# A down projection in seven products: sums left in their PSUM banks, and five steps of operands ready

## The chip, the core and the metric

The kernel runs on one core of a Trainium2 chip. TensorE multiplies matrices into PSUM, VectorE, ScalarE and POOL (GpSimd) do the rest, and SyncE's queue issues nearly all transfers. The metric is the time of one execution on the device, in microseconds (us).

## The reference

One layer of a bidirectional encoder over 1024 tokens of width 1024, in float32: a mixer, then a gated feed-forward block, then a last norm. The change touches only the end, the product of the gated activations with w_down, the addition to h and the last norm:

```
up = h @ w_up                                  # (1024, 5632)
conv = conv_b + sum_k conv_w[k] * padded[:, k:k + L]
gate, val = split(conv, 2)                     # each (1024, 2816)
y = h + (gelu(gate) * val) @ w_down            # w_down: (2816, 1024)
return rmsnorm(y, g_final)
```

## The kernel before

Each float32 operand is split into a high and a low part, by a ScalarE copy (L151) and a VectorE subtraction (L152), and each product of two operands is three matmuls: high by high, high by low, low by high.

The up projection runs over 22 blocks of 128 columns (`up_pair`); the gated block j is stored to DRAM as `adr[j]`. The down projection takes these blocks back as its stationary operand. It is a Strassen-Winograd scheme: both matrices are cut in two in each direction, and the four quarters of the result come out of seven products in place of eight. Rows 0 to 3 of the result (s = 0..3, 128 tokens each) and rows 4 to 7 are the two halves of the tokens, n = 0 and 1 the two halves of the columns.

Each product (`down(p, acc, ...)`) has KH = 11 steps m. A step loads one block of activations and one of weights (`d_<m>a`, `d_<m>b`, 256 KB each), splits both (`ringed`, a ring of 12 operands, so six steps ahead at most) and issues 12 matmuls: three for each of four banks. Products use the four banks `qa` or the four banks `qb`. `fresh` says whether the first matmul overwrites the bank; without it the product adds to what is there. Each product's operands are sums or differences of quarters. chain_a and chain_b hold them from one product to the next: begin_b and begin_a load two blocks for each step and subtract or add (L1223, L1219), and later products go on from there (L1228 in place, L1213 into the loaded tile).

Products one, two, five, six, seven, four and three run in this order. After product one, take_1 copies the banks to `u2` (ScalarE). Product two adds to the same banks; take_2 adds them to hb, the rows of h with the result (VectorE). Product five goes to qb; take_5 adds it. Product six overwrites qa; take_6 adds the banks to u2 (VectorE), and POOL adds u2 to three quarters of hb (L1329 to L1331). Product seven overwrites qa; take_7 adds it to hb. Product four adds to seven's banks, and its rows 4 to 7 are finished by out_rows; product three adds to five's banks, its last four steps are done bank by bank (tail 4), and rows 0 to 3 are finished by out_rows: addition, squares, rstd_of, POOL's product with g_final (L1291), scaling, store.

The operands of the first three steps of product one are loaded by load_first while the last up block is computed, in buffers of their own (`first`). Steps three and on take theirs from the pool that follows, whose memory comes free only with the up projection's. All loads of weights and blocks keep the order of the program on SyncE's queue (`st_load`). The order of instructions on each engine is fixed when the program is built, by a planner with its own simulated times; an engine runs its list in order.

Of the kernel before, what the change touches and what calls it, by code (L numbers as in the profile page):

```python
# [11 lines left out]
F32 = mybir.dt.float32  # L12
F32R = mybir.dt.float32r
I32 = mybir.dt.int32
BF16 = mybir.dt.bfloat16
AF = mybir.ActivationFunctionType
# [4 lines left out]
P = 128  # L21
L = 1024
D = 1024
NS = 8
# [9 lines left out]
NWP = 5  # L34
# [47 lines left out]
def bc(ap, axis, n):  # L82
    ap = ap.unsqueeze(axis)
    shape = list(ap.shape)
    shape[axis] = n
    return ap.broadcast_to(shape)
# [3 lines left out]
def encoder_block(  # L90
# [8 lines left out]
    V, A, PE, GP = nc.vector, nc.scalar, nc.tensor, nc.gpsimd  # L99
# [5 lines left out]
    outer = ctx.enter_context(tc.tile_pool(name="outer", bufs=1))  # L105
# [10 lines left out]
    def bank(name):  # L116
        return ps.tile([P, 512], F32, name=name, tag="bank_a")

    def bank2(name):
        return ps.tile([P, 512], F32, name=name, tag="bank_b")  # L120
# [8 lines left out]
    def mm(o, lhsT, rhs, start, stop, key=None, skip=False):  # L129
        i = PE.matmul(o, lhsT, rhs, start=start, stop=stop, skip_group_check=skip)  # L130
        last_mm[0] = i
        if key is not None:
            if key in chain:
                after(i, chain[key])
            chain[key] = i
        return i
# [13 lines left out]
    def split(dst_hi, dst_lo, src, eng=V):  # L150
        A.activation(dst_hi, src, AF.Copy)  # L151
        return eng.tensor_sub(dst_lo, src, dst_hi.bitcast(F32))  # L152
# [3 lines left out]
    def st_load(i):  # L156
        if st_chain:
            after(i, st_chain[-1])
        st_chain.append(i)

    def load_split(src, a, name, w=None, eng=V, g=None, geng=None):

        st = outer.tile([P, 512], F32, name=name + "_st", tag="st", bufs=5)
        sv = st.rearrange("p (a b) -> p a b", a=a) if a > 1 else st
        st_load(nc.sync.dma_start(sv, src))
        if g is not None:
            if geng == "A":
                for k in range(a):
                    A.activation(sv[:, k], sv[:, k], AF.Copy, scale=g[:, k:k + 1])
            else:  # L170
                geng.tensor_mul(sv, sv, bc(g, 2, P))
        if w is None:
            w = outer.tile([P, 2, 512], F32R, name=name, tag="wp", bufs=NWP)
        split(w[:, 0], w[:, 1], st, eng)
        return w.rearrange("p t (a b) -> p t a b", a=a) if a > 1 else w
# [7 lines left out]
    def rstd_of(ss, name, parts=0):  # L183

        v = const.tile([P, 1], F32, name=name + "_v", tag="rs_v", bufs=4)
        V.tensor_scalar(v, ss[:, 0:1], -0.5 / D, -0.5 * EPS, ALU.mult, ALU.add)
        for i in range(1, parts):
            V.tensor_scalar(v, ss[:, i:i + 1], -0.5 / D, v, ALU.mult, ALU.add)  # L188
        y = const.tile([P, 1], F32, name=name + "_y", tag="rs_y", bufs=4)
        t = const.tile([P, 1], F32, name=name + "_t", tag="rs_t", bufs=4)  # L190
        V.tensor_scalar(y.bitcast(I32), v.bitcast(I32), -0.5, float(0x5F3759DF - 0x40400000), ALU.mult, ALU.add)  # L191
        for _ in range(3):
            V.tensor_scalar(t, y, y, v, ALU.mult, ALU.mult)  # L193
            V.tensor_scalar(y, t, 1.5, y, ALU.add, ALU.mult)  # L194
        return y
# [770 lines left out]
    def cv_tile(name):  # L966
        return fp.tile([P, L], F32, name=name, tag="cv", bufs=2)
# [7 lines left out]
    for n in range(2):  # L975
        ns_ = slice(n * 512, (n + 1) * 512)
        for m in range(4):
            pg = bank(f"pg{m}_{n}")
            first = True
            for k in range(4):  # L980
                for wi, zi in ((0, 0), (0, 1), (1, 0)):
                    mm(pg, wg[k][:, wi, m * P:(m + 1) * P], zf[:, k, zi, ns_],
                       start=first, stop=(k == 3 and wi == 1))
                    first = False
# [78 lines left out]
    def halves(name):  # L1063
        t = cv_tile(name)
        return t[:, 0:512], t[:, 512:1024]
# [93 lines left out]
    first = []  # L1159
# [33 lines left out]
    def ringed(t, name):  # L1193
        w = pb.tile([P, 2, 512], F32R, name=name, tag="wr", bufs=12)
        split(w[:, 0], w[:, 1], t)
        return w
# [51 lines left out]
    hbs = {}  # L1248
    ss3 = {}
# [4 lines left out]
        ss3[s] = pb.tile([P, 4], F32, name=f"n3_{s}_s2")  # L1254

    def step(p, m):
        if p == 1 and m < 3:
            return first[2 * m], first[2 * m + 1]
        return tuple(ringed(f(m, f"d{p}_{m}{'ab'[i]}"), f"d{p}_{m}{'ab'[i]}o") for i, f in enumerate(forms[p]))

    def down(p, acc, fresh, more, extra=None, tail=1, done=None):

        groups = [(m,) for m in range(KH - tail)] + [tuple(range(KH - tail, KH))]
        for ms in groups:
            ops = []
            for m in ms:
                ops.append((m, *step(p, m)))
                if extra is not None:
                    extra(m)
            for si in range(4):  # L1270
                for m, a, w in ops:
                    for ai, wi in ((0, 0), (0, 1), (1, 0)):
                        mm(acc[si], a[:, ai, si * P:(si + 1) * P], w[:, wi], start=(fresh and m == 0 and ai == 0 and wi == 0),
                           stop=(m == KH - 1 and ai == 1), skip=more)
                if done is not None and ms[-1] == KH - 1:
                    done(si)

    def hv(s, n):
        return hbs[s][:, n * 512:(n + 1) * 512]

    def squares(s, n):
        sq = pb.tile([P, 512], F32, name=f"n3_{s}_sq{n}", tag="sq", bufs=2)
        A.activation(sq, hv(s, n), AF.Square, accum_out=ss3[s][:, n:n + 1])

    def out_rows(s, late, acc):

        end = s == 3
        o = pb.tile([P, L], F32, name=f"o{s}", tag="o", bufs=3)
        early = 1 - late
        el, ll = (slice(512 * n, 512 * n + 512) for n in (early, late))  # L1290
        GP.tensor_mul(o[:, el], hv(s, early), gl[:, el])  # L1291
        if end:
            for i, (c0, c1) in enumerate(((512, 768), (768, 1024))):
                V.tensor_add(hbs[s][:, c0:c1], hbs[s][:, c0:c1], acc[:, c0 - 512:c1 - 512])
                sq = pb.tile([P, 512], F32, name=f"n3_{s}_sq{2 + i}", tag="sq", bufs=2)
                A.activation(sq[:, 0:256], hbs[s][:, c0:c1], AF.Square, accum_out=ss3[s][:, 1 + i:2 + i])  # L1296
            r = rstd_of(ss3[s], f"n3_{s}", 3)
            A.activation(o[:, el], o[:, el], AF.Copy, scale=r)  # L1298
            nc.scalar.dma_start(ov[s][:, el], o[:, el])
            V.scalar_tensor_tensor(o[:, ll], hv(s, late), r, gl[:, ll], ALU.mult, ALU.mult)  # L1300
            nc.sync.dma_start(ov[s][:, ll], o[:, ll])
            return
        V.tensor_add(hv(s, late), hv(s, late), acc)
        squares(s, late)
        r = rstd_of(ss3[s], f"n3_{s}", 2)
        A.activation(o[:, el], o[:, el], AF.Copy, scale=r)
        V.scalar_tensor_tensor(o[:, ll], hv(s, late), r, gl[:, ll], ALU.mult, ALU.mult)  # L1307
        nc.sync.dma_start(ov[s], o)

    u2 = [h for i in range(2) for h in halves(f"du{i}")]  # L1310
    qa = [bank(f"dqa{si}") for si in range(4)]
    qb = [bank2(f"dqb{si}") for si in range(4)]

    def add_to(s, n, t):
        V.tensor_add(hv(s, n), hv(s, n), t)

    def take_1(si):
        A.activation(u2[si], qa[si], AF.Copy)

    def take_2(si):  # L1320
        add_to(si, 0, qa[si])
        squares(si, 0)

    def take_5(si):
        add_to(4 + si, 1, qb[si])

    def take_6(si):
        V.tensor_add(u2[si], u2[si], qa[si])
        GP.tensor_add(hv(4 + si, 0), hv(4 + si, 0), u2[si])  # L1329
        GP.tensor_add(hv(4 + si, 1), hv(4 + si, 1), u2[si])  # L1330
        GP.tensor_add(hv(si, 1), hv(si, 1), u2[si])  # L1331

    def take_7(si):
        add_to(4 + si, 1, qa[si])
        squares(4 + si, 1)

    def with_1(m):
        if m < 6:
            begin_b(m)
# [14 lines left out]
        if m % 2 and m < 8:  # L1354
            load_row(4 + m // 2)

    def after_6(si):
        take_5(si)
        take_6(si)

    down(1, qa, True, True, with_1, 1, take_1)
    down(2, qa, False, True, with_2)
    down(5, qb, True, True, with_5, 1, take_2)
    down(6, qa, True, False, with_6, 1, after_6)
    down(7, qa, True, True, None, 1, take_7)
    down(4, qa, False, True, None, 1, lambda si: out_rows(4 + si, 0, qa[si]))
    down(3, qb, False, True, None, 4, lambda si: out_rows(si, 1, qb[si]))


_INS = ['x', 'g_mix', 'w_in', 'ssm_lam_re', 'ssm_lam_im', 'ssm_log_dt', 'ssm_b_re', 'ssm_b_im', 'ssm_c_re',  # L1370
# [58 lines left out]
```

## Time and profile before

| | |
|---|---|
| median of 3 runs | 1081.42 us (1079.25 to 1083.48) |
| profiled execution | 1079.52 us, span 1077.7 us |
| TensorE (PE) | busy 975.3 us, 90% |
| VectorE (DVE) | busy 945.1 us, 88% |
| ScalarE (ACT) | busy 464.6 us, 43% |
| POOL | busy 252.2 us, 23% |

The span runs from the first to the last instruction in the trace. The time of an execution lies a little above it. Busy shares are means over stages with different limits; the down projection is the last 236 us.

### The profile page before, as it was taken

How to read it: one execution, taken by the hardware profiler on the slowest of the kernel's cores; microseconds unless marked ns; L12 is line 12 of the kernel's file. 1: busy time of each engine (PE TensorE's matmuls, PEld its weight loads, DVE VectorE, ACT ScalarE, POOL GpSimd, SP SyncE). 2: the span in 40 equal slices, each digit the busy share in tenths (PEclk: the TensorE clock that was granted, in tenths of full speed). 3: DMA queues.
4: the chain of work that ended last, by engine and by line, in shares of the span. 5: the costliest groups of instructions: out<-in, count | busy, mean ns of one | idle time of the engine just before them, and what ended most of it. 6: DMA issues, size and time to landing. Idle time of an engine off the chain costs nothing. (4 is left out here: it accounts for less than half of the span.)

```text
span 1077.7 us, 13528 instructions
## 1 busy us (share of the span) xinstructions
PE 975.3 (90%) x4504; PEld 803.1 (75%) x4504; DVE 945.1 (88%) x1717; ACT 464.6 (43%) x845; POOL 252.2 (23%) x255
## 2 busy tenths in 40 slices
PE   2798788778989999999999999999999699999796
PEld 1687666767767887788888888888877488887585
DVE  6898989999997899999988888988887678999796
ACT  5443223523124566444454444445453365434353
POOL 6247556766652003100000000000000000015103
PEclk9999988886999999999999999999999899999899
DMA  7261002342012323323223232222330899834623
GB/s 239 39 165 55 23 20 89 105 146 78 5 59 79 108 79 117 91 83 120 88 69 99 78 98 72 74 89 79 98 108 20 319 353 375 279 99 150 203 97 156
DMA packets 121596, 126.78 MB, mean 118 GB/s; under 512 B 17922, under 2 KB 86455, under 8 KB 121527
## 3 DMA queue, kind: packets, MB, share of 16 engines
q1 hardware_dynamic: 121382, 125.66, 36.2%
q8 instruction: 35, 0.57, 0.2%
q14 instruction: 35, 0.28, 0.1%
q10 hardware_dynamic: 144, 0.26, 0.1%
HBM read 103.35 MB, written 22.51 MB: 117 GB/s over the span
## 5 line engine op out<-in xcount | busy, mean ns | idle before, releaser
L130 PE MATMUL u<-xb,wo 128*128 128x512 f32 x528 | 129.9, 390 | 0.2
L1329 POOL TENSOR_TENSOR hb<-hb,du 128x512 f32<-128x512 f32 x4 | 6.9, 1713 | 526.8 <-DMA d_8a<-adr 526.8
L130 PEld LDWEIGHTS u<-xb,wo 128*128 128x128 f32 x528 | 99.0, 188 | 21.7 <-ACT xb L151 0.6
L130 PE MATMUL u<-xa,wo 128*128 128x512 f32 x408 | 98.8, 390 | 1.7 <-ACT ug L1117 1.5
L130 PEld LDWEIGHTS u<-xa,wo 128*128 128x128 f32 x408 | 76.4, 188 | 18.3 <-ACT ug L1117 1.9
L151 ACT ACTIVATE wo<-wu 128x512 fp32r<-128x512 f32 x78 | 49.1, 630 | 86.0 <-PE u L130 58.5
L130 PE MATMUL pin<-xh,win 128*128 128x512 f32 x256 | 79.1, 410 | 1.0 <-ACT xh L224 1.0
L1103 DVE SCALAR_TENSOR_TENSOR cg<-ug,cw,cg 128x896 f32<-128x896 f32 (+1 forms) x88 | 62.2, 747 | 13.9 <-ACT cg L1100 13.9
L130 PE MATMUL u<-t4o,wo 128*128 128x512 f32 x264 | 63.4, 389 | 0.0
L1103 DVE SCALAR_TENSOR_TENSOR cv<-uv,cw,cv 128x896 f32<-128x896 f32 (+1 forms) x88 | 62.1, 746 | 0.0
L151 ACT ACTIVATE wo<-ws 128x512 fp32r<-128x512 f32 x32 | 20.2, 631 | 90.3 <-PE u L130 81.9
L130 PE MATMUL pwo<-wo,yf 128*128 128x512 f32 x192 | 52.8, 423 | 5.7 <-DVE h L928 5.2
L130 PEld LDWEIGHTS pin<-xh,win 128*128 128x128 f32 x256 | 49.5, 197 | 11.2 <-ACT xh L224 1.5
L130 PEld LDWEIGHTS u<-t4o,wo 128*128 128x128 f32 x264 | 49.6, 188 | 10.3
L152 DVE TENSOR_TENSOR wo<-wu,wo 128x512 fp32r<-128x512 f32 x78 | 54.7, 701 | 0.0
L130 PE MATMUL u<-t1o,wx 128*128 128x512 f32 x204 | 49.5, 389 | 0.0
L130 PE MATMUL u<-t2o,wx 128*128 128x512 f32 x204 | 49.5, 389 | 0.0
L130 PEld LDWEIGHTS pwo<-wo,yf 128*128 128x128 f32 x192 | 37.4, 204 | 14.9 <-DVE h L928 6.3
L130 PE MATMUL pin<-xl,win 128*128 128x512 f32 x128 | 46.4, 411 | 0.1
L130 PEld LDWEIGHTS u<-t2o,wx 128*128 128x128 f32 x204 | 38.3, 188 | 7.9
L130 PEld LDWEIGHTS u<-t1o,wx 128*128 128x128 f32 x204 | 38.3, 188 | 7.9
L711 ACT ACTIVATE wt<-wt 128x128 f32<-128x128 f32 x32 | 9.9, 309 | 65.0 <-POOL wt L709 42.6
(558 smaller groups left out, 2489.6 us busy)
## 6 DMA issues: line engine op xcount, KB each, us to landing
wu<-in_w_up_dram SPq DMA_DIRECT2D x88, 256.0 KB, 3.0
adr<-cg SPq DMA_DIRECT2D x22, 512.0 KB, 3.0
xr<-in_x_dram SPq DMA_DIRECT2D x8, 512.0 KB, 8.0
win_st<-in_w_in_dram SPq DMA_DIRECT2D x16, 256.0 KB, 2.9
wo_st<-in_w_out_dram SPq DMA_DIRECT2D x16, 256.0 KB, 3.0
h<-in_x_dram SPq DMA_DIRECT2D x8, 512.0 KB, 4.6
hdr<-h SPq DMA_DIRECT2D x8, 512.0 KB, 2.6
hb<-hdr SPq DMA_DIRECT2D x8, 512.0 KB, 6.1
```

The source lines that it names most:

```text
L130: i = PE.matmul(o, lhsT, rhs, start=start, stop=stop, skip_group_check=skip)
L151: A.activation(dst_hi, src, AF.Copy)
L152: return eng.tensor_sub(dst_lo, src, dst_hi.bitcast(F32))
L711: A.activation(wf[:, :, 0:64], wf[:, :, 127:63:-1], AF.Copy, scale=(-1.0 if i else 1.0))
L1103: V.scalar_tensor_tensor(cv[:, lo:hi], src[:, at:at + hi - lo], w, cv[:, lo:hi], ALU.mult, ALU.add)
L1329: GP.tensor_add(hv(4 + si, 0), hv(4 + si, 0), u2[si])
```

## The change

Sums stay in their banks. Product two now goes to qb and take_2 adds it to the copy of product one (now `p1`). Product five overwrites qb. Product six adds to product one in qa; take_6 copies the sum to u2 (ScalarE, in two buffers of the ring wp); take_5 now comes after product six. Product seven adds to that in qa. Product three then adds to five in qb and finishes rows 0 to 3; during its first eight steps with_3 adds p1 and u2 to hb on VectorE and takes squares. Product four is last, adds to qa, has the tail of 4 and finishes rows 4 to 7. POOL's twelve additions are gone. The operands of steps three and four of product one are loaded by load_split into the buffers st and wp of the up projection.

```diff
     def step(p, m):
-        if p == 1 and m < 3:
+        if p == 1 and m < 5:
             return first[2 * m], first[2 * m + 1]
...
-        end = s == 3
+        end = s == NS - 1
...
-            for i, (c0, c1) in enumerate(((512, 768), (768, 1024))):
-                V.tensor_add(hbs[s][:, c0:c1], hbs[s][:, c0:c1], acc[:, c0 - 512:c1 - 512])
+            for i, (c0, c1) in enumerate(((0, 256), (256, 512))):
+                V.tensor_add(hbs[s][:, c0:c1], hbs[s][:, c0:c1], acc[:, c0:c1])
...
-    u2 = [h for i in range(2) for h in halves(f"du{i}")]
+    p1 = [h for i in range(2) for h in halves(f"dp{i}")]
+    u2 = []
...
     def take_1(si):
-        A.activation(u2[si], qa[si], AF.Copy)
+        A.activation(p1[si], qa[si], AF.Copy)
 
     def take_2(si):
-        add_to(si, 0, qa[si])
-        squares(si, 0)
+        V.tensor_add(p1[si], p1[si], qb[si])
...
     def take_6(si):
-        V.tensor_add(u2[si], u2[si], qa[si])
-        GP.tensor_add(hv(4 + si, 0), hv(4 + si, 0), u2[si])
-        GP.tensor_add(hv(4 + si, 1), hv(4 + si, 1), u2[si])
-        GP.tensor_add(hv(si, 1), hv(si, 1), u2[si])
+        A.activation(u2[si], qa[si], AF.Copy)
...
+    def with_3(m):
+        if m < 4:
+            add_to(m, 0, p1[m])
+            squares(m, 0)
+        elif m < 8:
+            add_to(m - 4, 1, u2[m - 4])
...
-    def after_6(si):
+    for m in (3, 4):
+        first.extend(load_split(src(0, 0, m), 1, f"d1_{m}{i}") for i, src in enumerate((act_src, wd_src)))
+    down(1, qa, True, True, with_1, 1, take_1)
+    down(2, qb, True, False, with_2, 1, take_2)
+    for i in range(2):
+        w = outer.tile([P, 2, 512], F32R, name=f"du{i}", tag="wp", bufs=NWP).bitcast(F32)
+        u2.extend((w[:, 0], w[:, 1]))
+    down(5, qb, True, True, with_5, 1)
+    down(6, qa, False, True, with_6, 1, take_6)
+    for si in range(4):
         take_5(si)
-        take_6(si)
-
-    down(1, qa, True, True, with_1, 1, take_1)
-    down(2, qa, False, True, with_2)
-    down(5, qb, True, True, with_5, 1, take_2)
-    down(6, qa, True, False, with_6, 1, after_6)
-    down(7, qa, True, True, None, 1, take_7)
-    down(4, qa, False, True, None, 1, lambda si: out_rows(4 + si, 0, qa[si]))
-    down(3, qb, False, True, None, 4, lambda si: out_rows(si, 1, qb[si]))
+    down(7, qa, False, True, None, 1, take_7)
+    down(3, qb, False, True, with_3, 1, lambda si: out_rows(si, 1, qb[si]))
+    down(4, qa, False, True, None, 4, lambda si: out_rows(4 + si, 0, qa[si]))
```

## Rows read from the trace of the kernel before

**Rows 1.** Windows of the down projection: window, length, busy by engine, clock, DMA share, GB/s

```profile
842.00:877.00 35.00, 25.40 (x100) 20.12 (x99) 27.06 (x41) 19.11 (x30) 0.00 (x0) 0.85 0.99 363
...
907.00:937.00 30.00, 30.00 (x134) 24.82 (x133) 29.71 (x50) 14.64 (x29) 0.00 (x0) 1.00 0.94 335
...
998.40:1038.50 40.10, 32.60 (x134) 26.78 (x134) 32.30 (x50) 16.10 (x32) 5.15 (x3) 0.87 0.60 190
...
1068.60:1077.70 9.10, 0.00 (x0) 0.00 (x0) 4.96 (x19) 2.63 (x7) 1.41 (x1) 0.73 0.44 173
```

**Rows 2.** All waits of TensorE from 830 us to the end: total, times, longest

```profile
PE dqa L130 <- ACT d_3bo L151: 9.0, 1, 9.0
PE dqa L130 <- DVE hb L1315: 7.5, 1, 7.5
PE dqa L130 <- DVE d_6bo L152: 1.5, 1, 1.5
PE dqa L130 <- DVE d_3bo L152: 0.6, 1, 0.6
```

**Rows 3.** Timeline of TensorE: start, length, operation, count, idle time before it

```profile
839.40 2.88 PE L130 MATMUL u<-xb,wo 128*128 128x512 f32 x12
851.28 2.08 PE L130 MATMUL dqa<-d_3bo,d_3ao 128*128 128x512 f32 x4 [9.00 <-ACT d_3bo L151]
...
876.71 0.84 PE L130 MATMUL dqa<-d_0bo,d_0ao 128*128 128x512 f32 x3
...
966.47 0.84 PE L130 MATMUL dqa<-d_0bo,d_0ao 128*128 128x512 f32 x3
...
995.54 2.88 PE L130 MATMUL dqa<-d_10bo,d_10ao 128*128 128x512 f32 x12
1005.92 1.62 PE L130 MATMUL dqa<-d_0bo,d_0ao 128*128 128x512 f32 x3 [7.50 <-DVE hb L1315]
...
1038.49 2.88 PE L130 MATMUL dqb<-d_0bo,d_0ao 128*128 128x512 f32 x12
...
1067.73 0.84 PE L130 MATMUL dqb<-d_10bo,d_10ao 128*128 128x512 f32 x3
```

**Rows 4.** Windows of 2 us around the two stops of TensorE, columns as above

```profile
846.00:848.00 2.00, 0.00 (x0) 0.00 (x0) 2.00 (x5) 0.00 (x0) 0.00 (x0) 0.87 1.05 389
...
856.00:858.00 2.00, 2.00 (x7) 1.59 (x6) 2.00 (x4) 0.64 (x1) 0.00 (x0) 0.57 1.04 404
...
1010.00:1012.00 2.00, 2.00 (x8) 1.59 (x7) 2.00 (x4) 1.36 (x5) 2.00 (x2) 0.67 0.50 176
```

**Rows 5.** Timeline around product one's start: SyncE's store, the last gelu, splits of d_5

```profile
817.49 18.34 SPq L1153 DMA_DIRECT2D adr<-cg  x2
...
849.13 1.06 ACT L1151 ACTIVATE cg<-cg 128x1024 f32<-128x1024 f32 x1 [3.66 <-DVE cg L1103]
...
854.58 0.63 ACT L151 ACTIVATE d_5ao<-d_5a 128x512 fp32r<-128x512 f32 x1 [1.40 <-DMA d_5a<-adr]
...
855.26 0.63 ACT L151 ACTIVATE d_5bo<-d_5b 128x512 fp32r<-128x512 f32 x1
```

**Rows 6.** POOL's groups of instructions, 842 to 1078 us: busy, mean ns, idle before

```profile
L1331 POOL TENSOR_TENSOR hb<-hb,du 128x512 f32<-128x512 f32 x4 | 7.0, 1739 | 0.0
```

**Rows 7.** Timeline of VectorE in product seven and at its end

```profile
969.24 1.27 DVE L1328 TENSOR_TENSOR du<-du,dqa 128x512 f32<-128x512 f32 x2
...
976.14 1.78 DVE L1213 TENSOR_TENSOR d_9b<-cb,d_9b 128x512 f32<-128x512 f32 x1
...
1002.68 0.69 DVE L1228 TENSOR_TENSOR cb<-d_8b,cb 128x512 f32<-128x512 f32 x1 [0.99 <-DMA d_8b<-in_w_down_dram]
...
1004.49 0.69 DVE L1228 TENSOR_TENSOR cb<-d_9b,cb 128x512 f32<-128x512 f32 x1
1005.10 0.68 DVE L1315 TENSOR_TENSOR hb<-hb,dqa 128x512 f32<-128x512 f32 x1
```

**Rows 8.** Timeline of VectorE behind product two: the last addition of take_2

```profile
912.01 0.68 DVE L1315 TENSOR_TENSOR hb<-hb,dqa 128x512 f32<-128x512 f32 x1
```

More of the change, by code (lines that the diff above doesn't have):

```diff
@@ L1292, in out_rows @@
         if end:
-            for i, (c0, c1) in enumerate(((512, 768), (768, 1024))):
-                V.tensor_add(hbs[s][:, c0:c1], hbs[s][:, c0:c1], acc[:, c0 - 512:c1 - 512])
+            for i, (c0, c1) in enumerate(((0, 256), (256, 512))):
+                V.tensor_add(hbs[s][:, c0:c1], hbs[s][:, c0:c1], acc[:, c0:c1])
                 sq = pb.tile([P, 512], F32, name=f"n3_{s}_sq{2 + i}", tag="sq", bufs=2)
-                A.activation(sq[:, 0:256], hbs[s][:, c0:c1], AF.Square, accum_out=ss3[s][:, 1 + i:2 + i])
+                A.activation(sq[:, 0:256], hbs[s][:, c0:c1], AF.Square, accum_out=ss3[s][:, 2 * i:2 * i + 1])
             r = rstd_of(ss3[s], f"n3_{s}", 3)
```

## Prediction

> **What bounds the kernel now.** I first cut the last 236 us, where the seven products of the down projection run, into stretches by product. TensorE is busy without a break in most of them and is not in two: product one keeps it busy for 25.40 of 35.0 us at a mean granted clock of 0.85, and product four for 32.60 of 40.1 us at 0.87 [rows 1]. Then I read TensorE's waits over the whole projection. The list has four rows and no more: 9.0 us for ScalarE's d_3bo, 7.5 us for VectorE's sum into hb, 1.5 us for d_6bo, 0.6 us for d_3bo's low part [rows 2]. Every other handover of a bank cost TensorE nothing, product one to two (behind a ScalarE copy) and six to seven (behind a VectorE addition) among them.
>
> TensorE's own timeline gives the yardstick. From the first matmul of product two (876.71) to that of product seven (966.47) lie 33 steps without a wait: 89.76 us, 2.72 us a step [rows 3]. Against it, product one is late: the last up product starts at 839.40 and its twelve matmuls would end at 842.12; the remaining eight steps end at 876.71 and not 842.12 + 21.76 = 863.88. Lost: 12.8 us. From product seven's start (966.47) to product three's (1038.49) 22 steps take 72.02 and not 59.84 us. Lost: 12.2 us. Product three is dense to the end, and the last matmuls begin at 1067.73 [rows 3]; behind them come 9.1 us of last additions, norm and output [rows 1]. The bound is therefore TensorE, with two holes of 25 us together.
>
> **First hole, steps three and four ready.** The operands of these steps are now loaded into buffers of the up projection, in order ahead of the loads for chain_b, and are split while the last up products run. Four loads, four ScalarE splits (0.63 each) and four VectorE subtractions move; their number stays the same. The cover for the splits is there: between 836 and 842 both engines are nearly idle, and I cost the move at nothing. Without the cover the four pairs would take some 5 us, of a wait that is there anyway. On SyncE's queue the four loads pass the store of block 20, at which it stands from 817.49 for 18 us [rows 5]: ahead of it they land early; behind it they push chain_b's first loads back by four issues of about 0.4 us, and d_5 still comes no later than now, as the same loads stand ahead of it.
>
> TensorE then has two more steps: 842.12 + 5.44 = 847.56. After that d_5 is late next. In the trace d_5a landed at 854.58, ScalarE having waited 1.40 us for it [rows 5]. Near there the DMA engines are full at 389 GB/s [rows 4], so a load of 262,144 bytes takes 0.67 us, and the four that no longer stand ahead of d_5 are worth 2.7: d_5a at 851.9, d_5b at 852.55 (0.67 later), its split done at 853.2. The gelu ahead on ScalarE ends at 850.2 [rows 5] and is no obstacle. So TensorE waits 5.6 us and resumes at 853.2.
>
> The clock: TensorE stopped at 842.1, and in 846 to 848 its granted clock fell to the lower level of 1.2 GHz (mean 0.87); after the restart at 851.28 the upper, 2.4 GHz, came back within 856 to 858 (mean 0.57, so near 857.7), and after that at 1005.92 within 1010 to 1012 (0.67, near 1011.3) [rows 3, 4]. A restart thus runs 5.4 to 6.4 us at half speed and loses 2.7 to 3.2 us. I take 2.9 for the new wait too, as it is longer than those 5 us of stop. Product one ends at 853.2 + 6 x 2.72 + 2.9 = 872.4 and not 876.7: **4.3 us gained**. Bounds: if d_5 lands as late as now, its split ends at 855.9 [rows 5] and the end is 875.1, gain 1.6; if the loads are as early as the gelu allows (two splits after 850.2: 851.4) and the clock holds, 867.7, gain 9.0.
>
> **Second hole, the banks.** Twelve POOL additions go (three like rows of four, 7.0, 6.9 and 6.9 us, of which one is shown [rows 6]; 20.8 us together), and the four VectorE additions of take_6. While POOL adds, VectorE's operand work with two SBUF inputs takes 1.78 us, where the next one starts 0.61 us later without it; an addition that reads PSUM stays at 0.64 (two in 1.27) [rows 7]. Some eleven such operations were stretched by 1.1 us: VectorE lost about 12 us, and TensorE's loss of 12.2 is that lag. It shows first as the wait for d_6bo (1.5), then in freed buffers that come late, so that VectorE waits for d_8b; the addition that frees the first bank for product four stands behind these and starts only at 1005.10 [rows 7], and TensorE, through with product seven near 998.3 (995.54 + 2.72), resumes at 1005.92, at the lower clock [rows 3]. 1.5 + 7.5 + 2.7 of clock gives 11.7 of the 12.2.
>
> With the new order product seven waits only for ScalarE's four copies of product six; such copies cost nothing between one and two [rows 2]. Product four comes after product three, so take_7 has 30 us for what now stops TensorE. **12.2 us gained**; bounds: 12.2, and 9 if the small waits around product seven stay.
>
> **What is added.** VectorE: eight additions in with_3 for the four of take_6, net 4 x 0.61 = 2.4 us. In product three that is four operations in a step of 2.72 us, 2.44 us, so hidden while VectorE leads; if it did not, 2.4 us. ScalarE: four copies more, 2.4 us, hidden in an engine that is under half busy. The new wait: product five writes the banks of product two, once take_2 has read them. VectorE is full there (29.71 of 30 us [rows 1]); in the trace the last of the four such additions starts at 912.01 [rows 8], 5.4 us after product two's end (876.71 + 11 x 2.72 = 906.63). If TensorE takes later steps of the banks already free, as it does elsewhere, it costs nothing; if not, the fourth bank (due 906.63 + 2.04) waits 4.0 us, with the clock 6.9. I take 0.5, since the like handover from six to seven shows no wait [rows 2]. Queued behind such a wait is all of TensorE. The tail keeps its form with another half of the columns: 0.
>
> **Sum.** -4.3 - 12.2 + 0.5 = -16.0 us. The profiled execution took 1079.52 us (span 1077.7), so 1063.5; the median of the three runs shown is 1.9 higher, and by it the result is 1065.4. I forecast **1064 us**, own range 1060 to 1068.
>
> **Rivals.**
> *The first part gains next to nothing* (17%): d_5 is no earlier, because the SyncE queue and not the bytes paces it. For it: before 846 the engines are not full. Against: 389 GB/s after. Gain 1.6 in place of 4.3: 1067.
>
> *The new handover from two to five stalls* (14%), with 6.9 in place of 0.5: 1070.5. For it: VectorE full, 912.01. Against: the list of waits.
>
> *VectorE loses more than it saves in product three* (5%). The additions moved into with_3 read two SBUF operands; those of take_2 that they partly replace read a bank. POOL's output multiplications (about as long as its additions) could now fall on them: eight stretched by 1.1 us are 9 us, with a fall of the clock 11.7: 1076, no measurable change. Against: only three of these can start before the first rows are written, as there are three output buffers. The Trainium skill (SBUF — State Buffer, "two separate sides") says that a VectorE operation with two SBUF inputs and a GpSimd operation exclude one another for a whole instruction; the 1.78 against 0.64 us agree, and by that rule every meeting costs VectorE about the rest of a POOL instruction, which speaks against with_3.
>
> *Each handover costs what the dear one did* (4%): TensorE stops at a bank until an in-order engine has read it, 7.5 + 2.9 = 10.4 us. The new order has four: two to five, six to seven, five to three, seven to four. All four are 41.6, less the 16.5 gained: 1105, slower. It decides from the third on (31.2 - 16.5 = 14.7). For it: one such handover is the 7.5. Against: the others had none [rows 2], and the last two come 30 us after the sums are complete.
>
> **The numbers.** Forecast 60%. The first two rivals are faster as well: 0.60 + 0.17 + 0.14 = 0.91, less 0.01 for their edge. Half a per cent (5.4 us) is about what a measurement of this kernel can tell from no change. Faster 0.90, same 0.06, slower 0.04. The range runs from 1058 (gain 9.0 at the start, no stall: 1079.5 - 21.2) to 1072 (second rival with the median's 1.9), and leaves out some 12 to 15 in 100.
>
> **What would show it.** Right: TensorE's 9.0 us wait becomes 5 to 6 us, on d_5 and not on d_3; no wait on hb; POOL without additions in product seven; VectorE's operations there at 0.6 us; products two to four at 29.9 us each; last matmul near 1052. Wrong: a wait on dp at product five's start or on du at product seven's, VectorE waited for near the end of product four, or d_5 landing at 854.

## The result, and the profile after

The changed kernel takes **1067.09 us** (median of 4 runs, 1066.99 to 1068.66) against 1082.31 for the kernel before in the same job: ratio 0.9867, 95% interval 0.9843 to 0.9891, about 14.4 us. Forecast were 1064 us and a range of 1058 to 1072. The profiled execution took 1066.99 us with a span of 1065.2, 12.5 less than before.

TensorE's waits over the whole down projection in the profile after (total, times, longest) have one row where [rows 2] has four:

```profile
PE dqa L130 <- ACT d_5bo L151: 8.5, 1, 8.5
```

TensorE's timeline after, from the last up products to the last matmul (start, length, operation, count, idle time before it); `dqa<-d,d` are the matmuls of the newly ready steps three and four:

```profile
829.48 1.52 PE L130 MATMUL dqa<-d,d 128*128 128x512 f32 x6
...
836.37 0.85 PE L130 MATMUL dqa<-d,d 128*128 128x512 f32 x3
...
839.10 0.84 PE L130 MATMUL dqa<-d,d 128*128 128x512 f32 x3
839.78 2.88 PE L130 MATMUL u<-t4o,wo 128*128 128x512 f32 x12
842.50 2.88 PE L130 MATMUL u<-xb,wo 128*128 128x512 f32 x12
845.22 2.88 PE L130 MATMUL dqa<-d,d 128*128 128x512 f32 x12
856.61 3.78 PE L130 MATMUL dqa<-d_5bo,d_5ao 128*128 128x512 f32 x8 [8.51 <-ACT d_5bo L151]
...
874.90 0.84 PE L130 MATMUL dqb<-d_0bo,d_0ao 128*128 128x512 f32 x3
...
904.82 0.84 PE L130 MATMUL dqb<-d_0bo,d_0ao 128*128 128x512 f32 x3
905.50 0.84 PE L130 MATMUL dqb<-d_1bo,d_1ao 128*128 128x512 f32 x3
...
994.58 0.61 PE L130 MATMUL dqb<-d_0bo,d_0ao 128*128 128x512 f32 x2
...
1053.74 0.84 PE L130 MATMUL dqa<-d_10bo,d_10ao 128*128 128x512 f32 x3
```

Product two begins at 874.90, product five at 904.82, and so on every 29.92 us: products six at 934.74, seven at 964.66, three at 994.58, four at 1024.50. From product two on nothing is lost. At 904.82 and 905.50 TensorE, at the new handover from two to five, takes steps 0 and 1 of a bank that is free while VectorE still reads the others.

The windows of the profile after (columns as in [rows 1]) say the same of product one, five, seven and the tail:

```profile
845.00:875.00 30.00, 21.49 (x87) 17.22 (x86) 23.81 (x36) 16.48 (x24) 0.00 (x0) 0.83 1.00 370
875.00:905.00 30.00, 30.00 (x134) 24.86 (x133) 22.09 (x36) 15.34 (x28) 0.00 (x0) 1.00 1.04 383
964.66:994.58 29.92, 29.92 (x134) 24.77 (x132) 27.72 (x46) 13.32 (x24) 0.00 (x0) 1.00 0.74 249
1053.74:1065.20 11.46, 0.84 (x4) 0.38 (x2) 7.06 (x26) 3.18 (x7) 1.26 (x1) 0.71 0.39 153
```

In the kernel before POOL's additions ran during product seven, and the stretch behind it (998.4 to 1038.5 in [rows 1]) had TensorE stopped and a mean clock of 0.87; now TensorE is busy at 1.00 through product seven, POOL is idle there, and the next products start 29.92 us apart. Only product one still has a hole. And the tail is longer: from the last matmul's start to the end of the span it takes 11.46 us, before 1077.7 - 1067.73 = 9.97.

VectorE in product seven after, with two-SBUF-input operations one behind the other at 0.60 us:

```profile
972.00 0.68 DVE L152 TENSOR_TENSOR d_5ao<-d_5a,d_5ao 128x512 fp32r<-128x512 f32 x1
972.60 0.68 DVE L152 TENSOR_TENSOR d_5bo<-d_5b,d_5bo 128x512 fp32r<-128x512 f32 x1
973.20 0.68 DVE L1213 TENSOR_TENSOR d_9a<-d_9a,ca 128x512 f32<-128x512 f32 x1
```

**Where the 12.5 us of span went.** The profiled execution after happens to run 1.72 us later than that of before where product one's ready matmuls begin (819.73 against 818.01, the second group of six), ahead of any matmul that the change adds; in the repeat of the changed kernel below the same matmuls start at 817.80. Product two begins at 874.90 in place of 876.71; with the 1.72 taken off, 3.5 us are gained there. Products two to four take 6 x 29.92; before, product seven to three lost 12.2 more: 12.2 gained. The tail loses 1.5. So -3.5 - 12.2 + 1.5 + 1.7 = -12.5.

### The profile page after: what moved, and what is told of

Same layout as the page of the kernel before. It is cut to its first block, busy times and chain, and to the rows that moved or that the text cites. A ratio compares the mean times of both kernels' runs of the same rounds, so it can differ in the third digit from the quotient of the medians.

```text
span 1065.2 us, 13505 instructions
## 1 busy us (share of the span) xinstructions
PE 971.2 (91%) x4504; PEld 800.6 (75%) x4504; DVE 934.3 (88%) x1721; ACT 466.2 (44%) x849; POOL 231.0 (22%) x243
## 5 line engine op out<-in xcount | busy, mean ns | idle before, releaser
L1291 POOL TENSOR_TENSOR o<-hb,gl 128x512 f32<-128x512 f32 x8 | 12.1, 1511 | 604.3 <-DVE hb L1316 470.0
L1103 DVE SCALAR_TENSOR_TENSOR cg<-ug,cw,cg 128x896 f32<-128x896 f32 (+1 forms) x88 | 62.2, 747 | 13.2 <-ACT cg L1100 13.2
L1103 DVE SCALAR_TENSOR_TENSOR cv<-uv,cw,cv 128x896 f32<-128x896 f32 (+1 forms) x88 | 62.0, 746 | 0.0
```

The lines of the kernel that those rows point to most:

```text
L1103: V.scalar_tensor_tensor(cv[:, lo:hi], src[:, at:at + hi - lo], w, cv[:, lo:hi], ALU.mult, ALU.add)
```

## The experiments

Ratios are to the kernel before, run on the same chip. "After" stands for the changed kernel, which was timed again beside the last two experiments.

> The changed kernel unaltered, beside the next two: 0.985 to 0.989 of the kernel before, TensorE's wait for d_5 8 to 9.5 us.

It took 1066.57 us, ratio 0.9863 (0.9846 to 0.9879), with a wait of 8.4 us on d_5bo and no other.

**One part alone: the five steps laid ready.** The kernel before with only

```diff
-        if p == 1 and m < 3:
+        if p == 1 and m < 5:
...
+    for m in (3, 4):
+        first.extend(load_split(src(0, 0, m), 1, f"d1_{m}{i}") for i, src in enumerate((act_src, wd_src)))
```

> Steps three and four of product one ready, banks and order as before. If the two parts of the change add up, product one ends 3 to 4.5 us earlier against the up projection's end, product four keeps its 7.5 us wait, and the time falls by 3 to 4.5 us. Rival: the 24 matmuls made ready only move TensorE's wait, the transfers behind them come as late as TensorE's last up product, and the time stays within 1 us.

Measured: 1078.33 us, 0.9975 (0.9963 to 0.9986), 2.7 us (1.5 to 4.0), a little below what was expected. TensorE's waits in this kernel:

```profile
PE dqa L130 <- ACT d_5bo L151: 9.3, 1, 9.3
PE dqa L130 <- DVE hb L1315: 8.6, 1, 8.6
PE dqa L130 <- DVE d_6bo L152: 1.2, 1, 1.2
PE dqa L130 <- DVE d_7bo L152: 0.4, 1, 0.4
```

The first wait is as long as before (9.0) and only two steps further on; the second hole is whole.

**The other part alone: the banks.** After, with `m < 3` again and without the two extra loads.

> Banks and order of the products as changed, steps three and four as before. If the parts add up: the 9.0 us wait of product one stays, no wait after it, some 12 us gained in products seven and four, about 1.5 us lost behind the last matmul: time lower by 10 to 12 us. Rival: the two parts need each other (without the earlier loads VectorE falls behind in product five): less than 8 us gained, with a wait for an addition into dp at product five's start.

Measured: 1069.98 us, 0.9899 (0.9881 to 0.9916), 10.9 us; the waits are those of product one in [rows 2] and a 1.5 in the up projection, which the kernel before has too (at 829.38), and none later. The parts add: 2.7 + 10.9 = 13.6 against the 14.4 of both.

**POOL's twelve additions given to VectorE.** The kernel before, its order and banks kept, three lines changed:

```diff
-        GP.tensor_add(hv(4 + si, 0), hv(4 + si, 0), u2[si])
-        GP.tensor_add(hv(4 + si, 1), hv(4 + si, 1), u2[si])
-        GP.tensor_add(hv(si, 1), hv(si, 1), u2[si])
+        V.tensor_add(hv(4 + si, 0), hv(4 + si, 0), u2[si])
+        V.tensor_add(hv(4 + si, 1), hv(4 + si, 1), u2[si])
+        V.tensor_add(hv(si, 1), hv(si, 1), u2[si])
```

> The kernel before, with POOL's twelve additions behind product six moved to VectorE. If POOL's additions cost VectorE some 11.5 us by stretching it, twelve additions of 0.61 us cost it 7.3 instead: the 12.2 us lost between product seven's start and product three's fall to about 8, time lower by 3 to 5 us. Rival: what counts is the work that stands ahead of the bank's readout on VectorE; then twelve more operations make the loss about 19 us and the time 5 to 7 us longer.

Measured: 1071.55 us, 0.9922 (0.9897 to 0.9946). It gains 8.4 us, more than I had expected, though VectorE has twelve more operations to do in the stretch in which it was late. Its profiled execution (1077.05) was its slowest of six, so only the stretch is read from it: product seven to product three takes 1036.03 - 970.24 = 65.8 us and not 72.0, a gain of 6.2 by these rows, and still 5.9 above the dense 59.84. TensorE's wait and what released it:

```profile
1003.15 1.62 PE L130 MATMUL dqa<-d_0bo,d_0ao 128*128 128x512 f32 x3 [2.83 <-DVE hb L1315]
```

The same wait as the 7.5 of [rows 2], now 2.8 us long.

**Product three ahead of four, POOL kept.** The kernel before, with POOL's additions and the old banks:

```diff
-    down(4, qa, False, True, None, 1, lambda si: out_rows(4 + si, 0, qa[si]))
-    down(3, qb, False, True, None, 4, lambda si: out_rows(si, 1, qb[si]))
+    down(3, qb, False, True, None, 1, lambda si: out_rows(si, 1, qb[si]))
+    down(4, qa, False, True, None, 4, lambda si: out_rows(4 + si, 0, qa[si]))
```

The last row's addition in out_rows moves to the other half of the columns with it, as in the change.

> The kernel before, POOL's additions kept, with product three ahead of product four (product four last with the tail of four steps). If VectorE's lag costs TensorE only at the bank that product four writes, 30 us more make it harmless: the 7.5 us wait and its low clock go, 1.5 us for d_6bo stays, time lower by 8 to 11 us. Rival: the lag itself is the cost, and product three waits for its operands instead: no more than 3 us gained.

Measured: 1081.35 us, 1.0000 (0.9985 to 1.0015): nothing. The wait on hb is gone, and others stand in its place, in products seven and four (two rows of the list of TensorE's waits):

```profile
PE dqa L130 <- DVE d_6bo L152: 2.5, 1, 2.5
PE dqa L130 <- DVE d_10bo L152: 2.4, 1, 2.4
```

Product seven to three takes 1003.73 - 969.33 = 34.4 us (4.5 lost), and the last product, 1033.65 to 1067.85, 34.2 where it took 1067.73 - 1038.49 = 29.24 in the kernel before. There VectorE does 1.76 us on an output row (L1307) while POOL does a later row's multiplication (L1291, from 1055.49), and d_10b's low part comes behind it at 1057.70. The tail behind the last matmul takes 1079.3 - 1067.85 = 11.45 us, 1.5 more than in the kernel before. So 4.5, 5.0 and 1.5 us have taken the place of the 12.2.

**POOL's load put back into the changed kernel.** After, with twelve POOL additions behind take_6's copies, whose results nobody reads:

```diff
         A.activation(u2[si], qa[si], AF.Copy)
+        for _ in range(3):
+            GP.tensor_add(scr, u2[si], hv(4 + si, 0))
```

> The changed kernel with twelve more POOL additions behind product six that read take_6's copy and a row of hb and write a buffer that nobody reads: the load on POOL of the kernel before without its place in the chain. If stretched VectorE operations are the cause, those of product seven take 1.78 us again and TensorE loses 5 to 12 us by waits for operands in products seven to four. Rival: POOL's additions cost only because others waited for the rows of hb; then VectorE's lag, if any, is hidden by its lead of six steps, and the time is that of the changed kernel within 2 us.

Measured: 1079.14 us, 0.9979 (0.9964 to 0.9994); some 12 us of the gain are gone. VectorE in product seven of this kernel, at the end of POOL's 12 additions (962.15 to 982.04):

```profile
977.50 1.75 DVE L1213 TENSOR_TENSOR d_8a<-d_8a,ca 128x512 f32<-128x512 f32 x1
...
980.84 1.75 DVE L1213 TENSOR_TENSOR d_8b<-cb,d_8b 128x512 f32<-128x512 f32 x1
982.51 0.68 DVE L152 TENSOR_TENSOR d_5ao<-d_5a,d_5ao 128x512 fp32r<-128x512 f32 x1
983.11 0.68 DVE L152 TENSOR_TENSOR d_5bo<-d_5b,d_5bo 128x512 fp32r<-128x512 f32 x1
```

and what TensorE makes of it:

```profile
983.85 5.06 PE L130 MATMUL dqa<-d_5bo,d_5ao 128*128 128x512 f32 x11 [7.01 <-DVE d_5bo L152]
```

An operation starts every 1.67 us up to POOL's last addition and every 0.60 behind it. No bank is waited for in this kernel; it is the operand d_5b that is late, and product seven to three takes 1002.55 - 962.85 = 39.7 us in place of 29.92. By these rows the additions cost 9.8 us; the profiled execution (1075.77) is one of this kernel's fastest.

**Chain_b's loads behind the steps.** After, with the six steps of begin_b at the end of product one and not at its start, so that d_5 and the steps behind it stand ahead of them on SyncE's queue:

```diff
     def with_1(m):
-        if m < 6:
-            begin_b(m)
+        if m >= 5:
+            begin_b(m - 5)
```

> The changed kernel, with the two loads of each of chain_b's first six steps moved behind the operands of steps five to ten of product one (they stood with steps zero to five). If the transfers ahead of d_5 set its time, d_5 needs only the row of g_final ahead of it: its splits start some 7 us earlier than 855.2, TensorE's 8.5 us wait falls below 2.5 us and the clock holds; time 6 to 10 us below the changed kernel, 20 to 24 below the kernel before. Rival: d_5 waits for memory that the last up product frees, or chain_b's loads, now between the steps, hold up steps six to ten: no more than 3 us below the changed kernel.

Measured: 1062.52 us, 0.9826 (0.9809 to 0.9843), 4.0 to 4.4 below after (0.9863, 0.9867), less than I had expected and more than the rival's 3. Rows from its trace, ScalarE, VectorE and TensorE:

```profile
847.76 0.61 ACT L151 ACTIVATE d_5ao<-d_5a 128x512 fp32r<-128x512 f32 x1
...
848.94 1.20 PE L130 MATMUL dqa<-d_5bo,d_5ao 128*128 128x512 f32 x4 [1.57 <-ACT d_5bo L151]
849.41 1.41 DVE L1103 SCALAR_TENSOR_TENSOR cg<-ug,cw,cg 128x127 f32<-128x127 f32 x2
850.73 0.69 DVE L152 TENSOR_TENSOR d_5ao<-d_5a,d_5ao 128x512 fp32r<-128x512 f32 x1
851.34 0.69 DVE L152 TENSOR_TENSOR d_5bo<-d_5b,d_5bo 128x512 fp32r<-128x512 f32 x1
...
852.08 3.78 PE L130 MATMUL dqa<-d_5bo,d_5ao 128*128 128x512 f32 x8 [1.94 <-DVE d_5bo L152]
```

d_5a's load is issued at 842.02 (after: 849.83) and its split runs 7.4 us earlier. The wait of 8.5 has become 1.6 + 1.9. But from the last up product's end, 841.77 + 2.72 = 844.49, to product two (870.10) it is 25.6 us against 29.7 after, only 4.1 less: the clock falls all the same (last section), and costs 3.1 of the 6.6 us that are still lost. d_5a's load now starts at the end of the same up product (u<-t4o,wo, 839.05 + 2.88 = 841.93) as the first load of bb did after, so the rival's wait for the up projection's memory is there as well, at another load.

**A fourth output buffer.** After, with `bufs=4` in place of 3 for the tile o.

> The changed kernel with four output buffers in place of three. If the last row's POOL multiplication, which waits for a buffer and then stretches a VectorE operation, costs the 1.5 us behind the last matmul, it now runs earlier: last matmul to the end of the span 9.3 to 9.8 us in place of 10.8, time 1 to 1.5 us below the changed kernel. Rival: the order of VectorE's list alone makes the tail longer, and the time stays.

Measured: 1066.96 us, 0.9872 (0.9854 to 0.9890), not told apart from after: the expected gain does not show in the time (in the profiled execution product one waits 9.2 us for d_5bo, after 8.5). The trace shows the effect on the tail all the same. VectorE in this kernel's last row (between the two halves of the addition):

```profile
1054.29 0.42 DVE L1294 TENSOR_TENSOR hb<-hb,dqa 128x256 f32<-128x256 f32 x1 [0.25 <-PE dqa L130]
1054.63 0.75 DVE L1307 SCALAR_TENSOR_TENSOR o<-hb,n_y,gl 128x512 f32<-128x512 f32 x1
1055.48 0.41 DVE L1294 TENSOR_TENSOR hb<-hb,dqa 128x256 f32<-128x256 f32 x1
```

and the same place in the profile after, where POOL stands beside it:

```profile
1054.62 0.42 DVE L1294 TENSOR_TENSOR hb<-hb,dqa 128x256 f32<-128x256 f32 x1 [0.31 <-PE dqa L130]
1054.92 1.26 POOL L1291 TENSOR_TENSOR o<-hb,gl 128x512 f32<-128x512 f32 x1 [5.70 <-DMA out_dram<-o]
1054.95 1.78 DVE L1307 SCALAR_TENSOR_TENSOR o<-hb,n_y,gl 128x512 f32<-128x512 f32 x1
1056.84 0.40 DVE L1294 TENSOR_TENSOR hb<-hb,dqa 128x256 f32<-128x256 f32 x1
```

With a fourth buffer POOL need not wait for a store, has multiplied earlier (the four of product four run from 1043.17 to 1049.93), and L1307 takes 0.75 us; the tail is 1063.9 - 1053.41 = 10.49 us and not 11.46 (9.8 from the end of the last matmul, the upper end of what was expected).

**Both, and g_final's load later.** chain_behind with four output buffers, and the load of g_final (`gl`, 1.49 us of SyncE's queue at 843.19 in the profile after, 0.38 in the kernel before) behind product two.

> The changed kernel with chain_b's first loads behind the operands of product one, four output buffers and the row of g_final loaded after product two. If the trace's terms add up (4.1 us before product two, 1.0 us behind the last matmul): 5 us below the changed kernel, 0.981 to 0.984 of the kernel before. Rival: the gains do not add up, since TensorE still waits for VectorE's low part of d_5: no more than 4 us below the changed kernel.

Measured: 1061.06 us, 0.9813 (0.9796 to 0.9830), 5.5 us below after's 1066.57 on the same chip. It is the fastest version here together with the next. The tail is 1058.2 - 1047.78 = 10.4 us; the waits in product one are 1.6 and 2.5.

**The last block's convolution behind product one.** As the one above, with the convolution, gelu and store of the last up block written in the program behind product one, so that its taps (L1103) should not stand ahead of d_5's low parts on VectorE.

> As the last one, with the convolution and gelu of the last up block emitted behind product one, so that VectorE's list may take the low parts of d_5 ahead of the convolution's taps. If the taps (1.41 us each) ahead of d_5's low part hold TensorE and let the clock fall, the 1.9 us wait and the half clock go: 3 to 5 us less than the last one, 0.977 to 0.980 of the kernel before. Rival: the planner keeps the taps where they are, or they stop ScalarE's splits instead: within 1.5 us of the last one.

Measured: 1060.49 us, 0.9813 (0.9797 to 0.9829): no change, and the same waits of 1.6 and 2.5. The planner put the taps where they had been (VectorE, this kernel):

```profile
846.08 1.41 DVE L1103 SCALAR_TENSOR_TENSOR cg<-ug,cw,cg 128x896 f32<-128x896 f32 x2 [1.37 <-ACT cg L1100]
847.41 1.41 DVE L1103 SCALAR_TENSOR_TENSOR cv<-uv,cw,cv 128x896 f32<-128x896 f32 x2
848.74 1.41 DVE L1103 SCALAR_TENSOR_TENSOR cg<-ug,cw,cg 128x127 f32<-128x127 f32 x2
850.06 0.69 DVE L152 TENSOR_TENSOR d_5ao<-d_5a,d_5ao 128x512 fp32r<-128x512 f32 x1
```

Three of four pairs are still ahead of d_5a. Whether the taps cost what is left of the hole is thus not tried by this kernel, and stays open.

## Why the prediction came out right, and where it did not

**The bound: right.** TensorE was the bound, with two holes. Away from the holes 29.92 us a product is all there is, and each part of the change did what it did at its own hole: alone 2.7 and 10.9 us. Of the prediction's signs of being right one failed: the wait on d_5 is 8.5 us and not 5 to 6.

**The second hole: size and mechanism right, one of its reasons wrong.** 12.2 us were predicted, and all 12.2 came. That POOL's additions stretch VectorE's work, and that this makes the lag, is shown from both sides: taken from POOL and given to VectorE itself, they cost 8.4 us less; put back into the changed kernel on POOL, they cost some 12 us, with the 1.67 us rhythm beginning and ending with POOL's stream. What the four additions saved on VectorE and the new order are worth once POOL's additions are gone, no run tries alone: with the twelve on VectorE and the order of before, 5.9 us are still lost. An operation that reads PSUM stayed at 0.64 in [rows 7]. The Trainium skill (SBUF — State Buffer, "two separate sides") says that a VectorE operation with two SBUF inputs and a GpSimd operation that reads SBUF shut one another out for a whole instruction; these runs agree, at 1.67 to 1.78 us against 0.60.

Wrong was the sentence that product four's new place frees take_7 of its stop, as if the place by itself were part of the gain. With the order turned and POOL kept, the time is that of before (1.0000): VectorE's lag then shows at d_6bo and, with POOL's output rows, at d_10bo. The 7.5 us on hb was the place where the lag came to light and not its cause. VectorE runs its list in order, and in these two kernels its lag was paid where its next result fell due.

**The first hole: the mechanism right, the term too large.** Predicted 4.3 us, in the trace 3.5, and 2.7 (1.5 to 4.0) for the part alone by its timing. The 3.5 is one pair of executions: from the first of product one's ready matmuls to product two the five profiles with five steps ready and chain_b's loads in front (after, its repeat, steps alone, POOL's load put back, fourth buffer) take 59.5 to 60.6 us, the four with three steps ready 62.6 to 63.8. Two steps of the term were off, in opposite directions. Predicted was that d_5a lands at 851.9, and that the moves cost nothing. It was waited for until 855.18, which is 853.5 with the 1.72 taken off. SyncE's queue after:

```profile
837.64 0.37 SPq L1190 DMA_DIRECT2D cb<-in_w_down_dram  x1
842.75 0.33 SPq L1190 DMA_DIRECT2D bb<-in_w_down_dram  x1
...
849.83 0.33 SPq L1190 DMA_DIRECT2D d_5a<-adr  x1
```

The first load of bb waits for memory that the up projection's products still use (SyncE waited 4.7 us for them, 3.3 before). It starts at 842.75, when the up product of 839.78 is through; in the kernel before it was 839.63. Of these 3.1 us 1.7 are the later run. The other 1.4 are the change's own: the planner put six of the ready steps' matmuls (two groups of three, at 836.37 and 839.10) ahead of the up product of 839.78, 6 x 0.227 = 1.36 us. Work that fills TensorE ahead of the hole thus put off the loads that end the hole. The wait was 8.5 us and not 5.6 for a second reason too: six more of the ready matmuls (829.48) fill a stop of the up projection that [rows 2], which begin at 830, leave out:

```profile
829.38 3.01 PE L130 MATMUL u<-xa,wo 128*128 128x512 f32 x12 [1.46 <-ACT ug L1117]
```

This is the kernel before; after, that up product has no wait. So TensorE comes to the hole 1.3 us sooner than predicted (847.94 - 1.72 = 846.2 and not 847.56), which lengthens the wait and costs nothing, as d_5 sets the restart. In the time of the kernel before the restart is at 856.61 - 1.72 = 854.9 and not 853.2. I had the four loads that went from d_5's queue, and not what the first of those left waits for.

The clock gave part back. 2.9 us were put down for it; TensorE restarts at 856.61, six steps of 2.72 would end at 872.93, and product two begins at 874.90, so it cost 2.0. Restart 1.7 late and clock 0.9 cheaper make 3.5 of the 4.3.

That the order of the loads on the queue kept d_5 late is shown by chain_behind: with d_5 ahead of chain_b's loads the 8.5 us of wait become 3.5. Of the 10.5 us of this hole (wait and clock) it leaves 6.6, and what would take these away no run shows.

**The handover from two to five: right.** 0.5 us were set aside, and it cost 0: as in the sentence ahead of it, TensorE took later steps of the banks already free (904.82, 905.50). That refutes the second rival, and the fourth too: none of the four new handovers has a wait.

**The first rival** (1.6 us in place of 4.3, 1067) is as near to the measured first part (2.7, 1.5 to 4.0) as the forecast; the time cannot part them. Its reason, that d_5 would be no earlier because the queue paces it, was half of what happened: d_5a was issued at 849.83 - 1.72 = 848.1 against 849.15, only 1.0 us earlier.

**The tail: not 0 but +1.5.** The step that failed is "the tail keeps its form". POOL's multiplication for the last row falls on VectorE's L1307 for an earlier one, which takes 1.78 us and stands between the two halves of the last addition; in the kernel before these two were back to back (0.74 us for both, from 1068.96). That is the third rival's mechanism, at a place where I hadn't looked, and at a sixth of its price. A fourth buffer takes back 1.0 of the 1.5. The longer tail comes with the order: it is 11.45 us in the kernel before with product three ahead of four, and 1076.2 - 1066.25 = 9.95 with the five steps alone. In product three, where that rival had put it, there is none of it: POOL is idle for 127.6 us up to 1042.13. The first three of its multiplications run in product five (906.80 to 914.50) and stretch three VectorE operations there to 1.46 to 1.78 us, without a wait of TensorE.

Sum: -3.5 - 12.2 + 0 + 1.5 = -14.2 by rows in place of -16.0, beside 14.4 by the ratio. The forecast of 1064 was off by the tail (1.5) and by the first hole (0.8), and the 0.5 set aside for the handover made up a part.

## What to carry to other kernels

An addition on POOL is not free if VectorE is full of two-SBUF-input work at the time: look at the mean of the same VectorE shape inside and outside POOL's stretches, and move POOL's work to a time when VectorE has slack, or leave the sums in PSUM, as here. A wait named in the list says where a lag falls due and not what made it; undo the suspected cause and keep the order, or the reverse, before crediting either. When operands are laid ready for TensorE, ask which loads wait for the matmuls that they now stand ahead of, and put the loads of the next step due ahead of those that are wanted later.

## What the runs showed of the hardware

TensorE's clock falls after quite different stops. In the kernel before it fell to 1.2 GHz within 846 to 848 [rows 4], and TensorE had stopped at 842.3 (851.28 - 9.00). In the profile after TensorE stopped at 848.1 (856.61 - 8.51) and it fell within 850 to 852. Windows of the profile after, columns as in [rows 1]:

```profile
850.00:852.00 2.00, 0.00 (x0) 0.00 (x0) 2.00 (x4) 0.00 (x0) 0.00 (x0) 0.57 1.05 393
...
860.00:862.00 2.00, 2.00 (x9) 1.58 (x9) 1.92 (x4) 1.18 (x2) 0.00 (x0) 0.87 1.03 400
```

In chain_behind it fell within 850 to 852 too, in the second of two waits, of 1.57 and 1.94 us, with four matmuls between them. Windows of chain_behind:

```profile
848.00:850.00 2.00, 1.06 (x4) 0.67 (x4) 2.00 (x5) 0.89 (x2) 0.00 (x0) 1.00 1.01 380
850.00:852.00 2.00, 0.14 (x1) 0.00 (x0) 2.00 (x4) 1.09 (x2) 0.00 (x0) 0.63 1.06 406
852.00:854.00 2.00, 1.92 (x5) 1.54 (x6) 2.00 (x5) 1.09 (x3) 0.00 (x0) 0.50 1.04 387
...
856.00:858.00 2.00, 2.00 (x7) 1.55 (x6) 2.00 (x3) 1.26 (x2) 0.00 (x0) 0.66 1.05 386
```

So a hole whose waits were cut from 8.5 us to 3.5 kept its whole price in clock: 870.10 - (847.21 + 6 x 2.72) = 6.6 us lost, of which 3.5 are waits and 3.1 the clock, where the long hole paid 2.0. How long the lower level lasts behind a restart differed as well: back within 860 to 862 after a restart at 856.61 in the profile after, within 856 to 858 after one at 851.28 in the kernel before.
